# First norm and head of the input projection as one hand-ordered region

## The chip, the cores and the metric

The kernel runs on one core of a Trainium2 chip. Its time is the time of one execution on the device in microseconds (us), the median of several runs. The profile shows one execution, instruction by instruction. TensorE (PE in the rows) multiplies; VectorE (DVE), ScalarE (ACT) and GpSimd (POOL) work on elements; SyncE (SP) here only issues loads.

## The reference, cut to what matters

The reference is a decoder trunk of two layers on an input of 512 tokens by 1024 channels, float32. Each layer normalizes its input, projects it onto the columns of four token mixers, runs these, projects back and adds; then it normalizes again, runs a gated convolutional feed-forward net, and adds. The part around the change is the first layer's start:

```
def rmsnorm(x, g):
    xf = x.astype(jnp.float32)
    y = xf * lax.rsqrt(jnp.mean(xf * xf, axis=-1, keepdims=True) + RMS_EPS)
    return (y * g).astype(x.dtype)
...
def reference(x, norm_mix, w_in, ...):
    for l in range(DEPTH):
        h = rmsnorm(x, norm_mix[l])
        proj = h @ w_in[l]
        pa, pb, pc, pd = split_cols(proj, [NSA_COLS, DIL_COLS, RWKV_COLS, CONV_COLS])
        ...
        x = x + jnp.concatenate([y_a, y_b, y_c, y_d], axis=-1) @ w_out[l]
        h = rmsnorm(x, norm_ffn[l])
        x = x + conv_ffn(h, ffn_up[l], ffn_dw[l], ffn_dw_b[l], ffn_down[l])
    return rmsnorm(x, norm_final)
```

## The kernel before, in words

Channels lie on the 128 partitions, so x is eight tiles of 128 channels by 512 tokens. Products are made in float16 from pairs: a weight tile is split into a high and a low part by ScalarE and VectorE (`_split`, L200 and L201), the normalized x into two parts likewise (`norm_apply`, L401 to L403), and `mm3` (L221 to L223) adds three products of the parts. An output tile of 128 channels takes 8 x 3 products of 512 columns.

The first norm works by halves of 256 tokens. `norm_add` squares each tile of x on ScalarE and adds the squares into two accumulators on VectorE and GpSimd. `norm_rb` sums the accumulators over channels with products by ones (L383), takes one over the root in ten small steps of VectorE (`rsqrt_cols`, L256 to L267), and spreads it over the channels with transposes (L387). `norm_apply` scales x, converts to the high part and subtracts for the low part. `gemm_head` makes the first four output tiles by halves of the tokens, in four banks of PSUM (two of a ring named g, two of a ring of three named r), and leaves them in `stash`, from which `rwkv_in` takes them. Evacuation of a bank is one operation of ScalarE and one of VectorE (L411, L412). The fifth tile needs a bank of the ring g again.

Staged weights have two buffers (`wst`), split weights five (`whl`). `next_w` keeps two weights ahead. x, one weight and the small tables are loaded in `run` under a raised priority, all of x through SyncE's queue; `layer_params` issues three small loads from ScalarE's queue and derives 12 small tables on GpSimd from the loaded parameters.

The order of each engine's instructions is not the order of the program: a planner draws it up with a model of the durations (`schedule_with_timeline_sim=True`), by priority and dependence. So loads, splits and products of different stages are interleaved, and parts of the second layer's parameters are loaded early.

## Time and profile before

| | us |
|---|---|
| median of three timed runs | 1356.83 |
| lowest and highest of them | 1355.47, 1357.44 |
| span of the profiled execution (first to last instruction) | 1353.0 |
| TensorE busy (share of the span) | 1301.1 (96%) |
| VectorE busy | 910.4 (67%) |
| ScalarE busy | 609.3 (45%) |
| GpSimd busy | 119.5 (9%) |

The profiled execution's own time is not given apart from its span; the timed runs lie 2.5 to 4.4 us above the span, their median 3.8. Busy time is the sum of the durations that the profile shows; products on TensorE overlap, and their ends are modelled, so a busy TensorE is not one at its peak. The spacing of two starts tells more of its pace than a duration.

### The profile page before, as it was taken

The numbers are of one execution on the slowest core, as the hardware profiler recorded it, in microseconds if no ns is written. First come the engines' busy times: TensorE is split into PE (matmuls) and PEld (weight loads), VectorE is DVE, ScalarE is ACT, GpSimd is POOL, SyncE is SP. The second block draws the span as 40 slices with busy tenths as digits, with TensorE's granted clock in tenths as the row PEclk, the third lists the DMA queues.
The fourth block names the chain that finished last, engine by engine and source line by source line (L and its number), as shares of the span: only waits on it lengthen the run. The fifth ranks groups of instructions, "written<-read, shape, count | busy, mean of one in ns | idle before, by whom it ended". The sixth has DMA issues, their size and how long they took to land.

```text
span 1353.0 us, 22896 instructions
## 1 busy us (share of the span) xinstructions
PE 1301.1 (96%) x9198; PEld 737.9 (55%) x9198; DVE 910.4 (67%) x1770; ACT 609.3 (45%) x1115; POOL 119.5 (9%) x180
## 2 busy tenths in 40 slices
PE   5999999999999999999999998999999999999996
PEld 4545567656644444444674455775584444444445
DVE  6779985777777777632277899757678677774323
ACT  5544567644544444422245345766345444443220
POOL 2000022213000000001100001223110000000110
PEclk9999989999999999999999999999999999999998
DMA  6521400022233233333333223001214333333321
GB/s 221 162 79 59 125 26 10 1 71 94 93 94 109 93 109 94 102 120 118 109 129 124 66 79 102 10 3 32 78 49 128 105 103 100 106 93 102 98 86 63
DMA packets 41866, 119.97 MB, mean 89 GB/s; under 512 B 4896, under 2 KB 11680, under 8 KB 41760
## 3 DMA queue, kind: packets, MB, share of 16 engines
q1 hardware_dynamic: 35136, 110.50, 26.2%
q10 hardware_dynamic: 6624, 8.01, 1.8%
q8 instruction: 72, 1.18, 0.4%
q14 instruction: 34, 0.28, 0.1%
HBM read 114.30 MB, written 4.19 MB: 88 GB/s over the span
## 4 chain that ended last, share of the span: by engine, by line
PE 77%; DVE 15%; ACT 3%; DMA 2%; issue 2%; SPq 0%; ACTq 0%; DVEq 0%
PE g L222 20%; PE g L223 20%; PE g L221 20%; DVE cacc L733 4%; DVE hl L201 3%; PE v L900 3%; PE t L889 2%; PE s L869 2%; PE r L556 1%; DMA st<-in_wi_dram 1%; ACT hl L200 1%; PE r L222 1%; PE r L223 1%; DVE e L872 1%; PE r L221 1%
## 5 line engine op out<-in xcount | busy, mean ns | idle before, releaser
L221 PE MATMUL g<-hx,hl 128*128 128x512 f16 (+1 forms) x1024 | 373.7, 368 | 4.2 <-ACT hx L402 3.7
L222 PE MATMUL g<-hx,hl 128*128 128x512 f16 (+1 forms) x1024 | 374.5, 368 | 1.0 <-DVE hx L403 0.9
L201 DVE SCALAR_TENSOR_TENSOR hl<-st,hl 128x1024 f16<-128x1024 f32 (+2 forms) x200 | 239.9, 1199 | 201.0 <-ACT hl L200 200.7
L223 PE MATMUL g<-hx,hl 128*128 128x512 f16 (+1 forms) x1024 | 374.9, 368 | 0.0
L200 ACT ACTIVATE hl<-st 128x1024 f16<-128x1024 f32 (+2 forms) x200 | 206.0, 1031 | 272.7 <-PE g L223 227.7
L221 PEld LDWEIGHTS <-hl 128*128 128x128 f16 x1724 | 170.6, 99 | 162.9 <-issue 7.5
L223 PEld LDWEIGHTS <-hl 128*128 128x128 f16 x1724 | 169.8, 98 | 157.8 <-issue 2.4
L222 PEld LDWEIGHTS <-hl 128*128 128x128 f16 x1724 | 170.2, 99 | 155.2 <-issue 2.9
L222 PE MATMUL g<-act,hl 128*128 128x512 f16 (+1 forms) x396 | 140.7, 355 | 0.0
L223 PE MATMUL g<-act,hl 128*128 128x512 f16 (+1 forms) x396 | 140.7, 355 | 0.0
L221 PE MATMUL g<-act,hl 128*128 128x512 f16 (+1 forms) x396 | 140.7, 355 | 0.0
L733 DVE SCALAR_TENSOR_TENSOR cacc<-gl,d_cdw,cacc 128x511 f32<-128x511 f32 (+14 forms) x120 | 89.8, 748 | 1.4
L370 POOL TENSOR_TENSOR acc<-acc,sq 128x256 f32<-128x256 f32 (+1 forms) x38 | 44.0, 1157 | 465.9 <-ACT sq L363 409.8
L887 POOL TENSOR_SCALAR e<-e,den 128x512 f32<-128x512 f32 (+3 forms) x96 | 55.9, 596 | 316.6 <-DVE den L879 208.0
L1006 DVE SCALAR_TENSOR_TENSOR x<-g,x 128x512 f32<-128x512 f32 (+1 forms) x62 | 34.9, 568 | 67.2 <-PE g L223 67.2
L1089 ACT CAST act<-u 128x512 f16<-128x512 f32 x44 | 27.2, 618 | 114.0 <-DVE u L1087 114.0
L872 DVE CUSTOM_DVE_ANT_0 e<-s,con 128x512 f32<-128x512 f32 (+3 forms) x96 | 46.7, 487 | 33.7 <-PE s L869 25.0
L1085 ACT ACTIVATE fth<-u 128x512 f32<-128x512 f32 x44 | 27.6, 628 | 82.9 <-DVE u L1082 82.9
L1082 DVE SCALAR_TENSOR_TENSOR u<-g,d_fdw,u 128x510 f32<-128x510 f32 x84 | 62.8, 748 | 2.7
L1080 ACT ACTIVATE u<-g,par,d_fdw 128x512 f32<-128x512 f32 x84 | 64.0, 762 | 0.0
L1081 DVE SCALAR_TENSOR_TENSOR u<-g,d_fdw,u 128x511 f32<-128x511 f32 x84 | 62.5, 744 | 0.0
L876 ACT ACTIVATE e<-e,mx 128x512 f32<-128x512 f32 (+3 forms) x96 | 53.2, 556 | 16.2 <-DVE mx L874 16.1
(265 smaller groups left out, 1634.3 us busy)
## 6 DMA issues: line engine op xcount, KB each, us to landing
st<-in_up_dram SPq DMA_DIRECT2D x88, 512.0 KB, 3.5
st<-in_wi_dram SPq DMA_DIRECT2D x40, 512.0 KB, 3.4
st<-in_dn_dram SPq DMA_DIRECT2D x32, 512.0 KB, 3.5
st<-in_wo_dram SPq DMA_DIRECT2D x16, 512.0 KB, 3.5
st<-in_dn_dram SPq DMA_DIRECT2D x16, 384.0 KB, 3.1
w<-in_cw_dram ACTq DMA_DIRECT2D x16, 256.0 KB, 4.1
st<-in_wv_dram SPq DMA_DIRECT2D x8, 396.0 KB, 3.1
x<-in_x_dram SPq DMA_DIRECT2D x16, 128.0 KB, 3.5
```

What stands on the lines that cost most here:

```text
L200: nc.scalar.activation(hl[:, 0, :cols], st[:, :cols], AF.Copy, scale=SW)
L201: nc.vector.scalar_tensor_tensor(hl[:, 1, :cols], st[:, :cols], SW, hl[:, 0, :cols], op0=ALU.mult, op1=ALU.subtract)
L221: nc.tensor.matmul(ps, hl[:, 0, w], hx[:, 0, cols], start=start, stop=False)
L222: nc.tensor.matmul(ps, hl[:, 0, w], hx[:, 1, cols], start=False, stop=False)
L223: nc.tensor.matmul(ps, hl[:, 1, w], hx[:, 0, cols], start=False, stop=stop)
L733: nc.vector.scalar_tensor_tensor(acc[:, s:512], gl[:, 0:512 - s], wj, acc[:, s:512], op0=ALU.mult, op1=ALU.add)
L872: nc.vector.tensor_tensor_reduce(es[i], ps[:, o:o + w], mask[:, 384 - 128 * t:512], op0=ALU.add, op1=ALU.max, scale=1.0, scalar=-3e38, acc ...
L876: nc.scalar.activation(es[i], es[i], AF.Exp, scale=SC, bias=mx[:, i:i + 1], accum_out=den[:, i:i + 1])
L887: nc.gpsimd.tensor_scalar(es[i], es[i], den[:, i:i + 1], 1.0, op0=ALU.mult, op1=ALU.mult)
L1080: nc.scalar.activation(u, ps, AF.Identity, scale=w[:, 88 + ch:89 + ch], bias=self.p("fb", ch))
L1081: stt(u[:, 1:512], ps[:, 0:511], w[:, 44 + ch:45 + ch], u[:, 1:512], op0=ALU.mult, op1=ALU.add)
L1082: stt(u[:, 2:512], ps[:, 0:510], w[:, ch:ch + 1], u[:, 2:512], op0=ALU.mult, op1=ALU.add)
```

## The change: what it does

`run` no longer loads x under raised priority and calls `norm_add` and `norm_apply`; it calls a new function, `open_x`, inside `tc.manual_schedule()`, within which each engine takes its instructions in the order of the program. In this region:

- The first halves of x are loaded by SyncE and ScalarE in turn. The first four weights have a staging buffer each (`st0`), all four loaded by SyncE between and behind the halves of x. The rest of the constants follows there, and the three small loads of `layer_loads` come at the region's end.
- 44, 28 and 8 products of a tile of zeros with itself are put on TensorE (`spin`): before the first half's sums, between them and the transposes, and behind the transposes.
- In the first half four squares are added by VectorE and two go straight to TensorE's sum. In the second half the six additions are on GpSimd.
- The subtractions of the second and fourth tile in the first half go to GpSimd.
- The first half's products go through two weights at once, then the third and the fourth; the second half's norm lies between. The second half's products go by tiles of x, all four weights for each.
- The first split behind the region is ordered behind the region's last conversion (ScalarE) and subtraction (VectorE).

`norm_rb` is cut into `norm_sums` and `norm_spread`, `_split` into `split_hi` and `split_lo`, `layer_params` into three, with the same instructions; the other changed lines are comments. The core of the diff:

```
     def gemm_head(self, hx, n):
+        if self.stash:
+            return
...
     def _split(self, src, cols):
-        nc.scalar.activation(hl[:, 0, :cols], st[:, :cols], AF.Copy, scale=SW)
-        nc.vector.scalar_tensor_tensor(hl[:, 1, :cols], st[:, :cols], SW, hl[:, 0, :cols],
-                                       op0=ALU.mult, op1=ALU.subtract)
+        first = self.split_hi(hl, st, cols), self.split_lo(hl, st, cols)
+        if self.opened is not None:
+            for later, earlier in zip(first, self.opened):
+                self.order(later, earlier)
+            self.opened = None
...
-        if l == 0:
-            self.nc.sync.dma_start(self.con[:, 128:], self.a["con"][:, 128:])
...
-            with tc.high_priority():
-                for i, cols in enumerate(self.HALVES):
-                    for k in range(NK):
-                        nc.sync.dma_start(self.x[k][:, cols], a["x"][:, k, cols])
-                    if i == 0:
-                        nc.sync.dma_start(self.con[:, :128], a["con"][:, :128])
-                        self.load_par(0)
-                    for _ in range(W_AHEAD):
-                        self.ready.append(self._split(*self.todo.pop(0)))
-            self.layer_params(0)
-            self.norm_begin(ip, 4, 2)
-            for cols in self.HALVES:
-                for k in range(NK):
-                    a1 = k % 3 == 1
-                    self.norm_add(k, cols, nc.gpsimd if a1 else nc.vector, int(a1))
-                self.norm_apply(self.d["gm"], hx, cols)
+            with tc.manual_schedule():
+                self.open_x(ip, hx)
...
+    def open_x(self, ip, hx):
+        nc, a = self.nc, self.a
+        h0, h1 = self.HALVES
+        load = lambda eng, k, cols: eng.dma_start(self.x[k][:, cols], a["x"][:, k, cols])
+        for k in range(NK):
+            load((nc.sync, nc.scalar)[k % 2], k, h0)
+        items = [self.todo.pop(0) for _ in range(HEAD)]
+        st = []
+
+        def w_in():
+            src, cols = items[len(st)]
+            t = ip.tile([128, 1024], F32, tag="st0", bufs=HEAD, name=self.n("st"))
+            nc.sync.dma_start(t, src)
+            st.append(t)
+
+        w_in()
+        nc.sync.dma_start(self.con[:, :128], a["con"][:, :128])
+        self.load_par(0)
+        w_in()
+        for k in range(NK):
+            load(nc.sync, k, h1)
+        w_in()
+        w_in()
+        nc.sync.dma_start(self.con[:, 128:], a["con"][:, 128:])
+        self.layer_consts()
+
+        idle = self.vbank()
+
+        def spin(n):
+            for _ in range(n):
+                nc.tensor.matmul(idle[:, 0:128], self.zero, self.zero, start=True, stop=True)
+
+        spin(44)
+        self.norm_begin(ip, 6, 2)
+        for k in range(NK):
+            self.norm_add(k, h0, nc.vector if k < NK - 2 else None, k % 2)
+        ps = self.norm_sums(h0)
+        spin(28)
+        hls = [self.whl.tile([128, 2, 1024], F16, tag="hl", name=self.n("hl")) for _ in range(HEAD)]
+        hi = lambda i: self.split_hi(hls[i], st[i], 1024)
+        lo = lambda i: self.split_lo(hls[i], st[i], 1024)
+
+        hi(0)
+        rb = self.norm_spread(ps, h0)
+        spin(8)
+        pss = [self.gbank() if i < BG else self.rbank() for i in range(HEAD)]
+
+        def mm(i, k, cols):
+            self.mm3(pss[i][:, cols], hls[i], k, hx[k], cols, k == 0, k == NK - 1)
+
+        def apply(rb, cols, pool, after):
+            nts = []
+            for k in range(NK + 1):
+                if k < NK:
+                    nts.append(self.norm_mul(k, self.d["gm"], rb, cols))
+                    act = nc.scalar.copy(hx[k][:, 0, cols], nts[k])
+                if k:
+                    dve = (nc.vector, nc.gpsimd)[k - 1 in pool].tensor_tensor(
+                        hx[k - 1][:, 1, cols], nts[k - 1], hx[k - 1][:, 0, cols], op=ALU.subtract)
+                    after(k - 1)
+            self.opened = act, dve
+
+        def first(k):
+            if k == 0:
+                lo(0)
+                hi(1)
+            if k == 2:
+                lo(1)
+            for i in {3: (0,), 4: (1, 2), 5: (3, 4), 6: (5, 6, 7)}.get(k, ()):
+                self.norm_add(i, h1, nc.gpsimd, i % 2)
+
+        apply(rb, h0, (1, 3), first)
+        for k in range(NK):
+            for i in range(2):
+                mm(i, k, h0)
+        for i in range(2, HEAD):
+            hi(i)
+            lo(i)
+        for k in range(NK):
+            mm(2, k, h0)
+        self.spread_done = None
+        ps = self.norm_sums(h1)
+        for k in range(NK // 2):
+            mm(3, k, h0)
+        rb = self.norm_spread(ps, h1)
+        for k in range(NK // 2, NK):
+            mm(3, k, h0)
+        apply(rb, h1, (), lambda k: None)
+        for k in range(NK):
+            for i in range(HEAD):
+                mm(i, k, h1)
+        self.layer_loads(0)
+        self.stash = pss
```

## Rows read from the trace of the kernel before

**Rows 1.** The page's first part: busy time, share of the span, instructions.
```profile
PE 1301.1 (96%) x9198; PEld 737.9 (55%) x9198; DVE 910.4 (67%) x1770; ACT 609.3 (45%) x1115; POOL 119.5 (9%) x180
```

**Rows 2.** Waits of TensorE, 45 to 1330 us: total, times, longest; first, last of 14.
```profile
PE v L936 <- DVE ec L933: 4.5, 2, 2.4
...
PE r L278 <- ACT yw L274: 0.2, 1, 0.2
```

**Rows 3.** Busy time by windows: PE, PEld, DVE, ACT, POOL, granted clock, DMA share, GB/s.
```profile
20.00:25.00 5.00, 5.00 (x34) 3.92 (x34) 4.96 (x17) 3.44 (x6) 0.00 (x0) 1.00 0.43 138
```

**Rows 4.** Timeline of TensorE, 8 to 48 us: start, duration, line, out<-in, idle before.
```profile
8.80 1.87 PE L383 MATMUL s<-ones,acc 128*128 128x1 f32 x8 [7.01 <-DVE acc L370]
16.28 0.69 PE L387 MATMUL t<-con,y 128*128 128x128 f32 x2 [5.62 <-DVE y L267]
...
20.09 0.42 PE L223 MATMUL g<-hx,hl 128*128 128x256 f16 x1
20.30 0.42 PE L221 MATMUL g<-hx,hl 128*128 128x256 f16 x1
...
22.86 0.28 PE L222 MATMUL g<-hx,hl 128*128 128x256 f16 x1
...
42.19 0.27 PE L223 MATMUL r<-hx,hl 128*128 128x256 f16 x1
42.30 0.38 PE L221 MATMUL g<-hx,hl 128*128 128x512 f16 x1
```

**Rows 5.** Timeline, 0 to 10 us: loads issued, and ScalarE's table load and last squares.
```profile
0.74 4.72 SPq L1178 DMA_DIRECT2D x<-in_x_dram  x8
...
1.66 0.45 ACTq L324 DMA_DIRECT2D pos<-in_pos_dram  x1
2.15 1.28 ACT L363 ACT_TABLE_LOAD   x1 [2.15 <-issue]
...
7.87 0.75 ACT L363 ACTIVATE sq<-x 128x256 f32<-128x256 f32 x2 [0.77 <-DMA x<-in_x_dram]
```

**Rows 6.** Timeline, 10 to 17 us: the root's steps, and an addition beside GpSimd's.
```profile
10.70 0.16 DVE L256 TENSOR_SCALAR u<-s 128x2 f32<-128x2 f32 x1 [1.96 <-PE s L383]
...
11.72 0.23 DVE L263 SCALAR_TENSOR_TENSOR y<-a,y 128x2 f32<-128x2 f32 x1
...
14.62 0.72 POOL L370 TENSOR_TENSOR acc<-acc,sq 128x256 f32<-128x256 f32 x1 [1.54 <-ACT sq L363]
...
14.78 0.85 DVE L370 TENSOR_TENSOR acc<-acc,sq 128x256 f32<-128x256 f32 x1
...
16.07 0.15 DVE L267 SCALAR_TENSOR_TENSOR y<-a,y 128x2 f32<-128x2 f32 x1
```

**Rows 7.** Timelines of ScalarE and VectorE: pace of squares, low parts, scalings, conversions, subtractions.
```profile
13.53 1.63 ACT L363 ACTIVATE sq<-x 128x256 f32<-128x256 f32 x5
...
27.80 1.23 DVE L201 SCALAR_TENSOR_TENSOR hl<-st,hl 128x1024 f16<-128x1024 f32 x1 [0.80 <-ACT hl L200]
...
30.16 1.26 DVE L401 SCALAR_TENSOR_TENSOR nt<-x,d_gm,t 128x256 f32<-128x256 f32 x3 [0.73 <-PE t L387]
30.68 1.19 ACT L402 CAST hx<-nt 128x256 f16<-128x256 f32 x3 [2.61 <-DVE nt L401]
31.35 0.75 DVE L403 TENSOR_TENSOR hx<-nt,hx 128x256 f16<-128x256 f32 x2
```

**Rows 8.** Timelines: weight load of zeros, and a later norm's sums.
```profile
16.55 0.15 PEld L378 LDWEIGHTS <-zero 128*128 128x128 f16 x1
...
323.16 0.50 PE L383 MATMUL s<-ones,sq 128*128 128x1 f32 x4
```

**Rows 9.** Timelines of ScalarE and VectorE: first evacuation, and a split behind it.
```profile
39.86 0.67 ACT L411 ACTIVATE wa<-g,d_om 128x512 f32<-128x512 f32 x1
40.43 1.05 ACT L200 ACTIVATE hl<-st 128x1024 f16<-128x1024 f32 x1
...
41.13 0.74 DVE L412 SCALAR_TENSOR_TENSOR wa<-g,d_mu,wa 128x511 f32<-128x511 f32 x1
```

More of the change, by code (lines that the diff above doesn't have):

```diff
@@ L191, in w_split @@
     def w_split(self, src, cols):
-        nc = self.nc
         with self.tc.high_priority():
@@ L196, in _split, with split_hi, split_lo @@
     def _split(self, src, cols):
-        nc = self.nc
         st = self.w_load(src, cols)
         hl = self.whl.tile([128, 2, 1024], F16, tag="hl", name=self.n("hl"))
-        nc.scalar.activation(hl[:, 0, :cols], st[:, :cols], AF.Copy, scale=SW)
-        nc.vector.scalar_tensor_tensor(hl[:, 1, :cols], st[:, :cols], SW, hl[:, 0, :cols],
-                                       op0=ALU.mult, op1=ALU.subtract)
-        return hl
+        first = self.split_hi(hl, st, cols), self.split_lo(hl, st, cols)
+        if self.opened is not None:
+            for later, earlier in zip(first, self.opened):
+                self.order(later, earlier)
+            self.opened = None
+        return hl
+    def split_hi(self, hl, st, cols):
+        return self.nc.scalar.activation(hl[:, 0, :cols], st[:, :cols], AF.Copy, scale=SW)
+    def split_lo(self, hl, st, cols):
+        return self.nc.vector.scalar_tensor_tensor(hl[:, 1, :cols], st[:, :cols], SW, hl[:, 0, :cols],
+                                                   op0=ALU.mult, op1=ALU.subtract)
     def plan(self, items, depth):
@@ L314, in layer_params, with ptile, layer_loads @@
     def layer_params(self, l):
-        nc, a = self.nc, self.a
-        t = lambda name, shape: self.cp.tile(shape, F32, tag=name, bufs=1, name=self.n(name))
-        if l:
-            self.load_par(l)
+        self.load_par(l)
+        self.layer_loads(l)
+        self.layer_consts()
+    def ptile(self, name, shape):
+        return self.cp.tile(shape, F32, tag=name, bufs=1, name=self.n(name))
+    def layer_loads(self, l):
+        nc, a, t = self.nc, self.a, self.ptile
         self.lora = t("lora", [128, 512])
@@ L324, in layer_params, with layer_consts @@
         nc.scalar.dma_start(self.pos, a["pos"][l])
-        v = nc.gpsimd
+    def layer_consts(self):
+        t = self.ptile
+        v = self.nc.gpsimd
         self.d = {}
@@ L373, in norm_rb, with norm_sums @@
         nc = self.nc
-        ps, rb = self.sbank(), self.tbank()
+        return self.norm_spread(self.norm_sums(cols), cols)
+    def norm_sums(self, cols):
+        nc = self.nc
+        ps = self.sbank()
         sqs = self.accs + self.direct
@@ L384, in norm_rb, with norm_spread @@
                                  start=False, stop=i == len(sqs) - 1 and t == n // 128 - 1)
+        return ps
+    def norm_spread(self, ps, cols):
+        nc = self.nc
+        rb = self.tbank()
+        n = cols.stop - cols.start
         y = self.rsqrt_cols("n", ps, n // 128, 1.0 / D, 1e-6)
@@ L394, in order, with norm_mul @@
             mybir.DependencyClass.NoSync, mybir.DependencyReason.DATA), reason="order")
+    def norm_mul(self, k, g, rb, cols):
+        t = self.np.tile([128, 256], F32, tag="nt", bufs=3, name=self.n("nt"))
+        self.nc.vector.scalar_tensor_tensor(t, self.x[k][:, cols], g[:, k:k + 1], rb, op0=ALU.mult, op1=ALU.mult)
+        return t
     def norm_apply(self, g, hx, cols):
@@ L399, in norm_apply @@
         for k in range(NK):
-            t = self.np.tile([128, 256], F32, tag="nt", bufs=3, name=self.n("nt"))
-            nc.vector.scalar_tensor_tensor(t, self.x[k][:, cols], g[:, k:k + 1], rb, op0=ALU.mult, op1=ALU.mult)
+            t = self.norm_mul(k, g, rb, cols)
             nc.scalar.copy(hx[k][:, 0, cols], t)
@@ L1214, in run @@
                         self.norm_apply(self.d["gm"], hx, cols)
+    def open_x(self, ip, hx):
[20 more added lines that the diff above has]
+        nc.sync.dma_start(self.con[:, 128:], a["con"][:, 128:])
+        self.layer_consts()
+        idle = self.vbank()
[58 more added lines that the diff above has]
+        self.stash = pss
```

## The prediction

> **What bounds the kernel now.** I read the page first: TensorE is busy for 96% of the span [rows 1], so a change pays only where it takes time out of TensorE's queue. The list of TensorE's waits inside the body, from 45 to 1330 us, has 14 rows that add up to 25.1 us, the longest group 4.5 us in two waits [rows 2]. The rest of TensorE's idle time lies at the two ends. So I went on to the timeline of the first 48 us. There the reader is to see three stretches. Until 20 us TensorE does nothing but two sums of squares and two pairs of transposes: it waits 7.0 us for the squares and 5.6 us for the root [rows 4]. From 20.09 the products of the first four output tiles follow each other without a hole until 42.30, when the fifth tile begins. In this stretch the 256-column products start 0.21 us apart at first and 0.11 us apart from about 22.9 us on. That is TensorE's two levels, 1.2 and 2.4 GHz, although the granted clock of 20 to 25 us reads 1.00 [rows 3, 4]: here I trust the spacing. What it did before the rise was dense products since 20.09, after some thin work.
>
> The yardstick is therefore one moment: the start of the fifth tile, 42.30 us. What comes later is not edited. The span is 1353.0 us and the median of the timed runs 1356.83, so some 3.8 us lie around the span; I carry them over unchanged.
>
> **The loads of x.** Before, SyncE issues the eight first halves in 4.72 us, 0.59 apart, and the last squares end at 8.62 [rows 5]. The last load was issued near 4.87, its square started near 8.2: 3.3 us from issue to use. Now four go through SyncE (the last at 0.74 + 3 x 0.59 = 2.51) and four through ScalarE's queue, where an issue took 0.45 and three ended at 2.11. The last x is there at 2.51 + 3.3 = 5.8. ScalarE's four issues end near 2.6, its table load takes 1.28, so squares start at 3.9; eight at 0.30 (five take 1.63, [rows 7]) end at 6.4 if nothing waits. I take 6.7: 1.9 us earlier than before. The three small tables that filled ScalarE's queue go to the end of the region, 1.4 us of issues behind the last conversion; they are wanted after the fifth tile, so that costs nothing. SyncE's later loads, the region's 4.2 MB of x and weights in all, are issued by 11 us at that spacing (17 issues behind 2.51, 0.5 each), and the third and fourth weight are wanted only near 20 us.
>
> **Products of zeros and sums of squares.** 44 products of 128 columns stand in TensorE's queue before the sums. The trace shows none back to back. Half the spacing of a 256-column product gives 0.107 us; the weight load of zeros takes 0.15 [rows 8], and if nothing overlaps one costs 0.26. So they end at 1.6 + 4.7 = 6.3, at 8.2, or at 13. I take the first, because in the dense stream the weight loads lie beside the products. The sums now have four operands in place of two: 16 records instead of 8. Eight took 1.87 us at the slow level [rows 4], four took 0.50 at the fast one, of which some 0.15 lies under the next product (a 256-column product lasts 0.27 at a spacing of 0.11) [rows 4, 8]. That is 3.7 or 1.5 us. With the clock risen by then, the sums end at 8.4; without, at 10.3.
>
> By the Trainium skill (TensorE: Matmul & The Clock Gate, "Back-to-back issue gap") a stream of 128-column products with their weight loads keeps about 81 ns each at the fast level. By it the 28 zero products behind the sums would take 2.3 us and hold the transposes back by 0.2 us, an estimate that I leave out of the sum; no run here shows it yet.
>
> **The root.** Six of its ten VectorE steps ran from 10.70 to 11.95, so ten take 2.05; but in the old order the weight's low part and additions came between, and the last ended at 16.22 [rows 6]. That interruption of 3.4 us goes. The root is ready at 10.5, the transposes (0.69 slow, half of it fast) end at 10.9. Before, they ended at 16.97. So the norm of the first half is 6.1 us earlier; call this moment t0.
>
> **What is late next.** The low parts of the weights, which the old order had made in the gap. VectorE's queue now holds four scalings (0.40), two subtractions (0.34) and two low parts (1.2) before the second weight is whole, with 0.4 of waits for ScalarE: t0 + 5.1. TensorE, in order, stands at the second tile's third product until then. The two tiles' 48 products then take 5.2 us at the fast level and are paced by the conversions to t0 + 9.8; if as many of them run at the slow level as did before, some 18 at 0.21, they end at t0 + 12.1. Between t0 - 1 and t0 + 5 TensorE does hardly 1.5 us of work, so I expect the slow level there. It matters little, since the third weight is late as well: ScalarE has eight conversions (0.39), the second high part (1.05), eight squares (0.30) and the third high part, 7.6 us, and some 3 us of waits for VectorE among them: t0 + 10.6, and the low part behind it t0 + 11.9. The third tile then ends at t0 + 14.6.
>
> Six additions of the second half's squares now stand on GpSimd, 0.72 each. A VectorE addition that began beside one of them took 0.85, more than two subtractions of that size in a row (0.75) [rows 6, 7], so they shut each other out: from the third square at t0 + 7.3, with two subtractions and two low parts between, they end near t0 + 14.6, just when TensorE comes to the sum. Unhindered they would end at t0 + 11.6.
>
> The rows show this of additions alone. The Trainium skill (SBUF — State Buffer, "SBUF: two separate sides") says which operations it holds for: VectorE's with two operands in SBUF against GpSimd's, each locked out for the whole of the other. By it the subtractions and the low parts of the weights lock as well and the scalings, with one operand in PSUM, do not; without it the additions on GpSimd would be 3 us earlier, and TensorE would still wait for the third weight, so the sum stays.
>
> Then 0.75 of sums, and the root (2.05) and transposes (0.35) beside 12 products (1.3): 0.75 idle. Twelve more, and the second half's 96 products at 0.109 run from about t0 + 19.7 to t0 + 30.4. Sum: 10.9 + 30.4 = 41.3.
>
> **The end of the region.** The old order finished the four tiles one after the other; now all four end in the last 1.3 us. The fifth tile needs the first one's bank, which is free after ScalarE's and VectorE's evacuation (0.67 and 0.74, [rows 9]). The first bank's last product is 0.98 before the end, so TensorE stands still for 0.5. If a weight's parts (1.05 and 1.2) are put ahead of the evacuation, which the old order also did, it is up to 2.0. I take 0.55: start of the fifth tile at 41.85 against 42.30, a gain of 0.45 us. That the rest of the order is drawn up anew by the planner I price at zero, with bounds from the waits it can move: one of the longest groups more or less, 4.5 us either way [rows 2].
>
> So the span becomes 1352.5 and the time 1356.4 us: the first norm comes 6.1 us earlier, and nearly all of it goes again in waits for weights, a late second norm and a bank. About 0.2%, 2.7 us, is what a measurement of this kernel can tell from no change.
>
> **Rivals.**
> The head gains more. If ScalarE and VectorE keep tighter than I count, the third weight is not late and the clock stays up, the second half ends near t0 + 27 = 37.9, and with 0.55 the gain is 3.9: 1353.0. For it: the zero products around the root. Against: ScalarE's queue as counted.
> The planner's new order of the body loses one of the long groups of waits: -0.45 - 4.4 gives 1352.0. Nothing in the profile speaks for it beyond the fact that such waits are few and single.
> The products of zeros stand in the way (slower). At 0.15 each they end at 8.2, and if the clock has not risen the sums take 3.7: 11.9 instead of 8.4, 3.5 later, and the transposes 0.35 more: 1360.2. It decides from 3.2 us on. For it: 0.15 of weight load at the slow level; against: dense products from 20.09 had brought the rise by 22.9 in the old order, and these start at 1.6.
> The bank (slower). Two weights' parts ahead of the first evacuation, and the second bank in the same queue: 4.5 us of standing instead of 0.55, 1360.3; it decides above 3.7. For it: a high part before the second evacuation at 40.43 [rows 9]; against: only one staging buffer is full by then.
> The change doesn't do what it says: that is nearly my forecast, the head ends when it did.
>
> **Chances.** Forecast 0.44 (own range 1354.4 to 1358.8), tighter head 0.17, better body 0.15, zeros in the way 0.11, bank or a worse body 0.13. Faster takes the two good cases, same the forecast, slower the two bad ones, with a little of each across the bounds: 0.33, 0.43, 0.24. The range 1351.6 to 1360.6 reaches the four rivals.
>
> **What would show it.** Right: squares done near 6.7, first transposes ended near 10.9, TensorE waiting on low parts of weights between 12 and 16 and again before the third tile, a hole of about half a microsecond before the fifth tile, and that tile starting within 1.5 us of 42.3. Wrong: first transposes after 13, the 256-column products 0.11 apart from 12 us on without holes, or waits in the body whose sum differs by more than 3 us.

## The result and the profile after

The changed kernel takes 1367.53 us (median of 4 runs, 1366.43 to 1370.56); the kernel before, run beside it, 1357.12. The ratio is 1.0088, 95% interval 1.0070 to 1.0106: slower by some 10 us where no change was forecast, and outside the range of the prediction.

The profiled run took 1368.60 us for a span of 1366.6; before, the span was 1353.0. The start of the fifth tile, the prediction's yardstick, and the four stretches behind it divide the 13.6 us between them. A stretch ends where the sums of the next norm are first read by VectorE.

| stretch, us | before | after | difference |
|---|---|---|---|
| to the fifth tile | 42.30 | 50.85 | +8.55 |
| first layer, mixers | 281.41 | 285.36 | +3.95 |
| first layer, feed-forward | 350.52 | 350.52 | 0 |
| second layer, mixers | 311.99 | 311.64 | -0.35 |
| second layer, feed-forward, and end | 366.78 | 368.23 | +1.45 |

So the head lost 8.55 us by itself, and the part that nobody edited, from here on "the body", lost 5.05. What lies around the span is 2.0 us in this run, not the 3.8 that the prediction carried over; by that the profile of before, with 1353.0, belongs to a run of about 1355.0. By the medians (+10.4) the body's share is 1.9.

TensorE's busy share is the same 96% [rows 1], and that tells nothing:

```profile
PE 1313.5 (96%) x9286; PEld 745.8 (55%) x9286; DVE 910.1 (67%) x1764; ACT 608.7 (45%) x1115; POOL 127.9 (9%) x184
```

**The loads.** The timeline of the changed kernel, first 20 us, DMA issues and ScalarE, then TensorE (start, duration, engine and line, out<-in; in brackets the idle time before and what ended it); it answers to [rows 4, 5]:

```profile
0.74 0.86 SPq L189 DMA_DIRECT2D st<-in_wi_dram  x2
1.65 4.20 SPq L1237 DMA_DIRECT2D x<-in_x_dram  x4
...
0.73 6.68 ACTq L1237 DMA_DIRECT2D x<-in_x_dram  x4
7.44 1.28 ACT L381 ACT_TABLE_LOAD   x1 [7.44 <-DMA st<-in_wi_dram]
...
9.37 1.94 ACT L381 ACTIVATE sq<-x 128x256 f32<-128x256 f32 x6
...
10.95 1.87 PE L405 MATMUL s<-ones,acc 128*128 128x1 f32 x8 [5.24 <-DVE acc L388]
12.68 1.85 PE L405 MATMUL s<-ones,sq 128*128 128x1 f32 x8
14.39 3.15 PE L1264 MATMUL v<-zero 128*128 128x128 f16 x28
17.33 0.63 PE L415 MATMUL t<-con,y 128*128 128x128 f32 x2
```

The reader is to see the first row. L189 is `w_load`: two weights of 512 KB, not of the region at all but of the fifth and sixth tile, stand at the head of SyncE's queue. The program issues them behind the region; the planner drew them ahead, since their staging buffers were free and nothing held them back. Everything behind them is late. The waits of SyncE's queue in the first 19 us (total, times, longest):

```profile
SPq L1237 <- DMA st<-in_wi_dram: 4.1, 3, 2.0
```

The trace names what holds an issue. All 290 transfers of the program signal their landing on eight semaphores, those of both queues together, and an issue that takes a semaphore again first waits until the transfer that had it has landed. So eight are in flight at most. Here the ninth and the tenth issue are the last x on SyncE's and on ScalarE's queue, and the semaphores that they take are those of the two weights. Timelines of SyncE (5 to 6 us) and ScalarE (6 to 7.4), and the time from issue to landing of the two weights (`--tile st`, 0 to 2 us):

```profile
5.52 0.33 SPq L1237 DMA_DIRECT2D x<-in_x_dram  x1
...
7.08 0.34 ACTq L1237 DMA_DIRECT2D x<-in_x_dram  x1
...
DMA to landing us min/median/max: 4.8/5.3/5.9
```

The weights were issued at 0.74 and 1.18 and landed at 5.50 and 7.06; each held issue follows 0.02 us behind a landing. So the four issues of x on ScalarE's own queue end at 7.41; the table load and the squares stand behind them, and the squares then follow each other without a wait. They end at 11.31, against 8.62 before and a forecast of 6.7. The loads of x also land late by themselves (the first at 5.67, in e1 below at 3.46); what the hold and what the shared transfer is worth is not told apart. The products of zeros had ended at 5.71, so TensorE then stood for 5.24 us, and the windows (columns as in [rows 3]; the number behind the five engines is the granted clock) show what followed:

```profile
5.00:10.00 5.00, 0.71 (x14) 0.59 (x11) 0.20 (x1) 2.55 (x6) 0.00 (x0) 0.81 0.84 275
10.00:15.00 5.00, 4.05 (x23) 4.05 (x24) 1.60 (x7) 2.36 (x6) 1.79 (x9) 0.50 1.00 304
```

From 10 to 15 us the granted clock is 0.50, the level of 1.2 GHz, though TensorE is busy for 4.05 of the 5 us: the 16 sums take 1.87 and 1.85 us and the 28 zeros 3.15.

**The bank.** The timeline around the fifth tile, ScalarE, VectorE, TensorE:

```profile
47.73 1.06 ACT L207 ACTIVATE hl<-st 128x1024 f16<-128x1024 f32 x1 [4.21 <-PE g L231]
48.70 0.67 ACT L443 ACTIVATE wa<-g,d_om 128x512 f32<-128x512 f32 x1
...
49.96 0.74 DVE L444 SCALAR_TENSOR_TENSOR wa<-g,d_mu,wa 128x511 f32<-128x511 f32 x1
...
50.85 0.38 PE L229 MATMUL g<-hx,hl 128*128 128x512 f16 x1 [2.18 <-DVE wa L444]
```

The planner put the sixth tile's split ahead of the first evacuation on both engines, 1.06 and 1.23 us, and the fifth tile waits 2.18.

**The body.** Waits of TensorE behind the head, 54 to 1340 us (total, times, longest); the same list as [rows 2], now 17 rows that add up to 28.3 us in place of 25.1:

```profile
PE v L968 <- DVE ec L965: 4.3, 2, 2.6
...
PE g L229 <- DVE u L1114: 2.2, 2, 1.6
...
PE r L288 <- ACT yw L284: 1.3, 2, 1.1
```

Before, the wait for `yw` was 0.2 [rows 2] and the one for `u` 0.6, in a row between those shown. Of the body's 5.05 us in this pair of profiles 3.2 are such waits.

### The profile page after: what moved, and what is told of

It reads as the page before. It is cut to its first block, busy times and chain, and to the rows that moved or that the text cites. A ratio compares the mean times of both kernels' runs of the same rounds, so it can differ in the third digit from the quotient of the medians.

```text
span 1366.6 us, 23065 instructions
## 1 busy us (share of the span) xinstructions
PE 1313.5 (96%) x9286; PEld 745.8 (55%) x9286; DVE 910.1 (67%) x1764; ACT 608.7 (45%) x1115; POOL 127.9 (9%) x184
## 4 chain that ended last, share of the span: by engine, by line
PE 75%; DVE 15%; ACT 4%; DMA 3%; issue 2%; ACTq 0%; DVEq 0%; SPq 0%
PE g L230 20%; PE g L231 20%; PE g L229 20%; DVE cacc L765 4%; DVE hl L210 3%; PE v L932 3%; DMA st<-in_wi_dram 2%; PE t L921 2%; PE s L901 2%; ACT hl L207 1%; PE r L588 1%; DVE e L904 1%; PE r L230 1%; PE r L231 1%; PE r L229 1%
## 5 line engine op out<-in xcount | busy, mean ns | idle before, releaser
L388 POOL TENSOR_TENSOR acc<-acc,sq 128x256 f32<-128x256 f32 (+1 forms) x40 | 47.6, 1194 | 460.5 <-ACT sq L381 404.4
```

## The experiments

All kernels ran beside the kernel before. "Head" is the start of the fifth tile less 42.30; "time" is the median less that of before in the same series; "body" is time less head; "mixers" is the first mixer stretch of the profiled run (281.41 before).

| kernel | transposes end | fifth tile | head | time (ratio, 95% interval) | body | mixers |
|---|---|---|---|---|---|---|
| changed | 17.96 | 50.85 | +8.55 | +10.4 (1.0070 to 1.0106) | 1.9 | 285.36 |
| e1 | 11.03 | 43.36 | +1.06 | +7.8 (1.0032 to 1.0065) | 6.8 | 288.18 |
| e2 | 17.80 | 49.05 | +6.75 | +14.9 (1.0092 to 1.0125) | 8.2 | 283.91 |
| e3 | 10.72 | 41.38 | -0.92 | +4.5 (1.0024 to 1.0043) | 5.4 | 283.17 |
| e4 | 12.73 | 45.11 | +2.81 | +15.5 (1.0093 to 1.0136) | 12.6 | 288.56 |
| e5 | 15.54 | 49.16 | +6.86 | +6.6 (1.0028 to 1.0053) | -0.2 | 281.92 |
| e6 | 10.74 | 41.00 | -1.30 | +8.0 (1.0034 to 1.0064) | 9.3 | 286.66 |
| e7 | 11.64 | 41.00 | -1.30 | +4.9 (1.0027 to 1.0055) | 6.2 | 285.24 |
| e8 | 21.05 | 47.15 | +4.85 | +5.1 (1.0021 to 1.0044) | 0.3 | 282.86 |
| e9 | 11.62 | 42.58 | +0.28 | +24.1 (1.0165 to 1.0200) | 23.8 | 293.62 |
| e10 | 16.54 | 41.67 | -0.63 | +27.6 (1.0184 to 1.0228) | 28.2 | 295.28 |
| e11 | 10.60 | 40.59 | -1.71 | +20.7 (1.0131 to 1.0165) | 22.4 | 290.29 |
| e12 | 11.59 | 42.53 | +0.23 | +5.2 (1.0024 to 1.0052) | 5.0 | 284.18 |
| e14 | 11.68 | 41.03 | -1.27 | +5.1 (1.0022 to 1.0046) | 6.4 | 285.19 |
| e21 | 11.34 | 40.69 | -1.61 | +16.7 (1.0094 to 1.0145) | 18.3 | 300.06 |
| e22 | 11.23 | 41.53 | -0.77 | +3.6 (1.0023 to 1.0049) | 4.4 | 285.99 |
| e24 | 16.15 | 41.83 | -0.47 | +19.2 (1.0127 to 1.0158) | 19.7 | 299.66 |

Head and mixers are read from one profiled execution each. e3, e9, e12 and e22 have the same region and heads from -0.92 to +0.28, so a head is known to about 1 us. Runs of one kernel lie up to 7.5 us from their median (e21: 1365.49, with a median of 1373.01), and the intervals of the ratios are 1.3 to 3.5 us to either side. A body is known to some 2 to 4 us.

### e1 to e3: the loads and the bank

e1 orders every weight load of `w_load` behind the region's last load; e2 orders the second split behind the region behind the first evacuation; e3 does both.

```
-        nc.sync.dma_start(st[:, :cols], src)
+        ld = nc.sync.dma_start(st[:, :cols], src)
+        if self.last_load is not None:
+            self.order(ld, self.last_load)
...
+        elif self.second and self.evac is not None:
+            for later, earlier in zip(first, self.evac):
+                self.order(later, earlier)
```

Expected of e1: 

> The two weights that the planner drew ahead of x on SyncE's queue (fifth and sixth tile) are put behind the region's last load. Theory (those two loads are the main loss: bandwidth, and issues of x that wait for them): last squares end near 6.8 us instead of 11.3, the sums run at the fast level, first transposes end near 11 instead of 18.0, the fifth tile starts near 44 instead of 50.85, time 1360 to 1361. Rival 1 (the order by hand sets the pace, x is early enough anyway): fifth tile not before 48, time 1365 or more. Rival 2 (the loss lies in the body's new order): the fifth tile moves but the time stays within 2 us of 1367.5.

Expected of e2: 

> The second weight behind the region is split behind the evacuation of the first bank, on ScalarE and VectorE, instead of ahead of it; nothing else. Theory (the bank is the smaller loss): TensorE's wait before the fifth tile falls from 2.2 to 0.6 us, fifth tile near 49.2, time near 1366. Rival (the evacuations are what holds the whole mixer stage): time 1363 or less. No effect if the split waits for something else as well: 1367.5.

Expected of e3: 

> Both edits. Theory: the gains add, first transposes end near 11, fifth tile near 42.3 as in the kernel before, and the time is what the body's order leaves: 1357 if it costs nothing, near 1360.5 if the 3.5 us that the changed kernel loses between the fifth tile and the feed-forward norm stay. Rival (one wait hides the other): not better than the first edit alone by more than 0.5 us.

The heads came out as expected, to 0.9 us. The timeline of e1, loads, table load and transposes:

```profile
0.73 1.81 SPq L1240 DMA_DIRECT2D x<-in_x_dram  x4
...
0.73 1.86 ACTq L1240 DMA_DIRECT2D x<-in_x_dram  x4
2.62 1.28 ACT L384 ACT_TABLE_LOAD   x1 [2.62 <-issue]
...
10.60 0.43 PE L418 MATMUL t<-con,y 128*128 128x128 f32 x2 [0.45 <-DVE y L280]
```

The same four issues on ScalarE's queue take 1.86 us in place of 6.68, and the transposes end 6.9 us earlier: the two loads alone had cost 7.5 us of head. In e1 the first eight issues are the eight loads of x; the ninth, a weight, goes at 3.47, and the last x lands at 6.33 in place of 9.20. e2 took the wait for the bank from 2.18 to 0.64. e3 has both, and its head is the one that was predicted:

```profile
4.55 2.33 ACT L391 ACTIVATE sq<-x 128x256 f32<-128x256 f32 x6
...
7.22 1.03 PE L415 MATMUL s<-ones,sq 128*128 128x1 f32 x8
8.12 1.72 PE L1276 MATMUL v<-zero 128*128 128x128 f16 x28
10.29 0.43 PE L425 MATMUL t<-con,y 128*128 128x128 f32 x2 [0.45 <-DVE y L287]
...
41.38 0.38 PE L239 MATMUL g<-hx,hl 128*128 128x512 f16 x1 [0.64 <-DVE wa L454]
```

The times missed for e1 by 2.4 to 3.4 us and for e2 by 4.5; e3 came in within its range, at the slow end. With the head mended the kernel is still 4.5 us slower than before, so a third cost lies in the body.

### e4: without the zeros

e1 with an empty `spin`; the products whose results nobody reads are left out.

Expected: 

> The loads put behind, as in the first, and no products of zeros at all. Theory (the zeros are worth the level of the sums and of the first products): the 16 records of the sums take 3.7 us instead of 1.5, transposes end near 13, fifth tile near 46, time near 1362.5. Rival (the clock falls again before the real products, so the zeros change nothing that counts): fifth tile within 0.7 us of the first experiment's.

```profile
6.31 1.87 PE L408 MATMUL s<-ones,acc 128*128 128x1 f32 x8 [4.53 <-DVE acc L391]
8.04 1.85 PE L408 MATMUL s<-ones,sq 128*128 128x1 f32 x8
...
12.04 0.69 PE L418 MATMUL t<-con,y 128*128 128x128 f32 x2 [2.15 <-DVE y L280]
```

The sums take 1.87 and 1.85 us in place of 1.03 each (e3), and the fifth tile is 1.75 later than in e1. So the zeros do what the change adds them for, where they reach to the sums. In the profiles of the kernels with the loads in order they don't always: in e1, e3, e6 and e11 the first 44 end between 6.30 and 6.47, when the sums begin, and the 28 behind the sums take 1.72 us; in e7, e9, e12, e14 and e21 they end between 5.49 and 5.80, TensorE stands for 0.3 to 0.7 us before the sums, and the 28 take 2.88 to 3.15 (e22 lies between, with 2.13). The granted clock from 8 to 12 us is 1.00 in e3 and 0.61 in e12, whose region is the same; that makes most of the difference between their heads. What ends the zeros early in one profile and not in another is not shown. The time is 7.6 us worse than that of e1, of which the head explains 1.75; the rest is the body again.

### e5: a head that is only longer

The kernel before with 64 more products by zeros inside the first four tiles (which adds nothing to them), to tell a later start of the body from a different body.

```
-                    self.mm3(ps[:, cols], hl, k, hx[k], cols, k == 0, k == NK - 1)
+                    self.mm3(ps[:, cols], hl, k, hx[k], cols, k == 0, k == NK - 1 and not longer)
+                    if longer:
+                        self.nc.tensor.matmul(ps[:, cols], self.zero, hx[k][:, 0, cols], start=False,
+                                              stop=k == NK - 1)
```

Expected: 

> The kernel before, with a 256-column product of zeros added to each of the 64 steps of the first four tiles: the head alone is made 64 x 0.109 = 7.0 us longer, the planner draws up the rest as it likes. Theory (the planner's new order behind a shifted head costs time by itself): from the fifth tile to the first sum of the feed-forward norm it takes 283 to 288 us instead of 281.4, or a feed-forward stage gets its 1.7 us longer; time 7 us and 2 to 6 more. Rival (a shift of the head passes through one to one, and the body's loss in the changed kernel comes from how its region ends): that stretch stays within 0.7 us of 281.4, time 7 us more.

The head is 6.86 later and the time 6.6; the first mixer stretch keeps its length to 0.5 us. The rival holds: a shift of the head passes one to one, and is no cause of a body cost. What e5 also keeps is the order: of TensorE's first 1600 products and transposes from the first `lora` product on, all but 2 lie in the longest sequence that it shares with the kernel before, compared by the tiles that each writes and reads. In the changed kernel 21 lie outside, in e1 to e7 without e5 36 to 39.

### e6, e7: banks in turn, and zeros ahead of the first products

e6 is e3 with the last half of the second half's channels tile by tile, so that the banks come free one after the other; e7 puts 14 and 20 more zeros ahead of the first products of the first and second tile.

```
-        for k in range(NK):
+        for k in range(NK // 2):
             for i in range(HEAD):
                 mm(i, k, h1)
+        for i in range(HEAD):
+            for k in range(NK // 2, NK):
+                mm(i, k, h1)
...
+                if k == 0:
+                    spin((14, 20)[i])
                 mm(i, k, h0)
```

Expected of e6: 

> Both edits of the third experiment, and the second half's products by tile from the fifth tile of x on, so that the four banks are finished 1.3 us apart instead of in the last 1.3 us together. Theory (the common end makes the wait for the bank): no wait before the fifth tile, which starts near 40.6 instead of 41.38. If the body's loss comes from the late splits and evacuations at the common end, the stretch up to the feed-forward norm falls back to 281.5 and the time to 1356; if it comes from the planner's order, the stretch takes some other value from 281 to 288.

Expected of e7: 

> As the experiment before, and 14 and 20 more products of zeros ahead of the first products of the first and the second weight, where TensorE waits for the low parts anyway. Theory (between root and second weight the clock falls): no 256-column product at a spacing of 0.21, against 21; the first two tiles end 2 us earlier, but the third weight's low part then ends the wait, so the fifth tile moves by 0.5 to 1.0 only. Rival (the slow products are the bound): it moves by 2.2.

e6 has no wait for the bank left, and its fifth tile starts at 41.00; in its profile the wait for the second weight's low part is longer (2.5 in place of 1.6). e7 has none of the 17 to 23 products at the slow spacing that e1, e3 and e6 show, and its fifth tile starts at 41.00 too. TensorE now waits 0.29 and 0.87 for the third weight's parts, which it didn't in e6. In e7's profile the transposes also end 0.9 later than in e6, with slow zeros before them; e11, whose region is the same, has its fifth tile at 40.59. So the gain is 0.4 us or less by the start of the fifth tile, 0.9 from the transposes on, and not the rival's 2.2. That is the prediction's "the third weight is late as well", and speaks against its rival of a tighter head.

### e8: the old order with x on two queues

The odd tiles of x's first half from ScalarE's queue, nothing else.

```
-                        nc.sync.dma_start(self.x[k][:, cols], a["x"][:, k, cols])
+                        (nc.sync, nc.scalar)[k % 2 * (1 - i)].dma_start(self.x[k][:, cols], a["x"][:, k, cols])
```

Expected: 

> The kernel before with one part of the change alone: the odd tiles of x's first half are loaded from ScalarE's queue. Theory (x's arrival sets the first norm): last squares end near 7.2 instead of 8.6, first root earlier by as much or less, since a weight's low part still stands between its steps; fifth tile 0.5 to 1.5 earlier, time within 2 us of before. Rival (the first weight's arrival sets the first products): fifth tile within 0.3.

A miss: the fifth tile is 4.85 later, not earlier.

```profile
1.18 3.00 ACTq L1178 DMA_DIRECT2D x<-in_x_dram  x4
...
5.84 1.28 ACT L363 ACT_TABLE_LOAD   x1 [5.84 <-DMA x<-in_x_dram]
```

ScalarE's queue here still had the three tables to issue, its issues of x took 3.00 us, and the table load came at 5.84 against 2.15 [rows 5]. An issuing queue that is also the engine of the squares pays for each held issue. The ninth issue, a load of x on ScalarE's queue, went at 3.85, when the load of x whose semaphore it takes had landed. The body kept its order (2 of 1600) and, by the medians, its length.

### e9 to e11: the chain of the compression moved

In e3 TensorE is idle for 1.3 us some 20 to 28 us behind the fifth tile (the 3.4 in the expectation of e9 is not in this trace), among the small products of `cmp_in`, here called links, each of which needs the one before. e9 (on e3), e10 (on the kernel before) and e11 (on e7) put that chain behind the next group of tiles in the program, in both layers. The expectations from here on take the first `r<-kvr,bk`, a product of the first mixer, as a mark of time.

```
-ORDER = ("R0 CM E0 R1 E1 ...
+ORDER = ("R0 CM E0 R1 CH2 E1 ...
```

Expected of e9: 

> The kernel of e3 with the chain of the compression (its small products behind the pooled keys, each waiting for the one before) put behind the second group of tiles in the program, so that the planner lays a tile between its links. Theory, the planner's new order costs the body its time: in e3 the links stand one behind another on TensorE, 3.4 us idle and a fall of the granted clock to 0.70 some 20 to 28 us behind the fifth tile; here links 3 and 4 lie between products, the first r<-kvr,bk starts at about +58.5 behind the fifth tile (e3: 60.8, before: 57.5), the first mixer stretch is 281.4 to 282.5 (e3: 283.2), the time about 1358.5 (e3: 1360.0). Rival, the loss comes from the granted clock or late weights whatever the order: +60.5 or more, 283 to 286, 1360 or more.

Expected of e10: 

> The kernel before with the same edit alone. Theory: its chain had tiles between its links already, so nothing is to be gained: within 1 us of before, first mixer stretch 281 to 282. Rival, the edit is a gain of its own: 2 us or more faster than before, which would say nothing of the region.

Expected of e11: 

> The kernel of e7 (loads in order, banks in turn, zeros ahead of the first products) with the same edit. Theory: the first r<-kvr,bk from +62.3 to about +58.5, the first mixer stretch from 285.2 to 281.5 to 282.5, the time from 1360.0 to about 1357. Rival: 284 to 286 and 1360.

All three are 20 to 28 us slower, the kernel before too. The control makes this a failed experiment, and the most telling one: an edit that I had priced at nothing costs 28 us behind an untouched head. 304 of 1600 products lie outside the shared sequence there, but in e9 only 56, so the count does not price an order. e9 loses 12 us in each layer's mixers (293.6 and 323.6 in place of 281.4 and 312.0). Whether the late chain itself or the new order is the cost, these runs do not tell.

### e12, e14: only the last links, by an order on TensorE

The last links behind the root's transposes, where TensorE has them in the kernel before; their lines also move there in the program, for all engines. e12 is on e3, e14 on e7. The same edit in the kernel before was not run.

```
+        if self.rest is not None:
+            self.rest()
...
+            self.order(mm, self.spread_end)
```

Expected of e12: 

> The kernel of e3 with the last links of the first layer's compression ordered, on TensorE alone, behind the transposes of the first mixer's root (r<-con,yw), which gives TensorE the order that it has in the kernel before: root, link, second lora pair, a tile, link, a tile, link. Theory, the planner draws the links ahead of the root and each is waited for in the open: waits of s on ACT part, DVE hid and ACT kc gone (1.6 us with the loads behind), the granted clock 1.00 from 20 to 32 us behind the fifth tile (e3: 0.70 in one stretch), the first r<-kvr,bk at +59 or less (e3: 60.8), first mixer stretch 281.4 to 282.3 (e3: 283.2), time 1358 to 1359 (e3: 1360.0). Rival, another wait takes the place (the root itself is late because ACT and DVE are): +60.5 and 283, time 1360.

Expected of e14: 

> The kernel of e7 with the same order of the links. In e7 they lie ahead of the root on VectorE (0.6 us) and ScalarE (four copies, 0.9 us), and the root's copy yw ends the wait of TensorE. Theory: the second lora pair from +26.6 behind the fifth tile to about +24.5, the first r<-kvr,bk from +62.3 to about 59.5, first mixer stretch from 285.2 to 282 to 283, time from 1360.0 to 1357 to 1358. Rival, the tile whose weight comes late is what TensorE lacks: +61.5 or more, 284 to 286, 1360.

My theory fell. The links' waits are gone, and the wait moved to the root's copy `yw`, which feeds the transposes, as the rival of e12 said. But e14's timeline names what is ahead of it (VectorE, ScalarE, TensorE):

```profile
53.69 1.22 DVE L495 TENSOR_TENSOR_SCAN lc<-rst,lw 128x512 f32<-128x512 f32 x1
...
57.22 1.06 ACT L218 ACTIVATE hl<-st 128x1024 f16<-128x1024 f32 x1 [4.24 <-DMA st<-in_wi_dram]
58.18 0.61 ACT L498 ACTIVATE pc<-lc 128x512 f32<-128x512 f32 x1
...
59.98 1.05 PE L270 MATMUL r<-con,sq 128*128 128x2 f32 x8 [0.82 <-ACT sq L506]
...
65.02 1.11 PE L299 MATMUL r<-con,yw 128*128 128x128 f32 x4 [2.98 <-ACT yw L295]
```

`lc` is ready at 54.9, but ScalarE stands for 4.24 us before a split whose weight has not landed, and `pc` is behind it. In the kernel before, ScalarE waits for `lc` there, and TensorE for nothing:

```profile
55.90 0.63 ACT L453 ACTIVATE pc<-lc 128x512 f32<-128x512 f32 x1 [3.98 <-DVE lc L450]
...
63.41 0.66 PE L278 MATMUL r<-con,yw 128*128 128x128 f32 x4
```

And the clock goes with it. Windows of e14: TensorE busy for 1.04 of 4 us, then the level of 1.2 GHz:

```profile
61.00:65.00 4.00, 1.04 (x33) 0.77 (x32) 2.81 (x11) 1.49 (x4) 0.00 (x0) 0.72 0.54 176
65.00:69.00 4.00, 3.98 (x12) 2.04 (x13) 3.37 (x6) 1.34 (x3) 0.00 (x0) 0.50 0.16 64
```

### e21, e22, e24: that split behind the stage's square

One order on ScalarE: the first split that follows the first mixer's elementwise stage in the program comes behind that stage's square. e21 on e7, e22 on e3, e24 on the kernel before.

```
+        if self.hold is not None and self.held is None:
+            self.order(first[0], self.hold)
+            self.held = self.hold
...
+        self.hold, self.held = act(sq, k, AF.Square, scale=self.p("k_k", c)), self.held or self.hold
```

Expected of e21: 

> The kernel of e7 with one added order in the first layer: the first split that follows the first mixer's elementwise stage in the program (the eighth tile's weight) comes on ScalarE behind that stage's square sq<-k, so the later splits do too. In e7 and e14 seven splits stand ahead of the exponential pc, the last of them waits 4.2 us for its load, and pc, sq, the sums, the root's copy yw and the evacuation of the sixth tile's bank follow it, so TensorE stands. Theory, splits drawn ahead of that stage cost the region's kernels their body time: sq by about +14 behind the fifth tile (e7: 18), second lora pair at about +22 (e7: 26.6), the first r<-kvr,bk at 57.5 to 59 (e7: 62.3), first mixer stretch 281 to 282.5 (e7: 285.2), time about 1356.5 (e7: 1360.0). Rival, TensorE runs out of work there whatever stands on ScalarE: 61.5 or more, 284 to 286, 1360.

Expected of e22: 

> The kernel of e3 with the same added order. Theory: the first r<-kvr,bk at 58 to 59.5 behind the fifth tile (e3: 60.8), first mixer stretch 281 to 282.5 (e3: 283.2 in its profile), time about 1357.5 (e3: 1360.0). Rival: 60.5 or more, 283 to 286, 1360.

Expected of e24: 

> The kernel before with the same added order alone: there the exponential waits for VectorE, not for a split (pc 3.98 us behind lc), so theory expects next to nothing: within 1 us of before, first r<-kvr,bk at 57 to 58.5, first mixer stretch 281 to 282. If it gains 2 us or more the order is a gain of its own and says less about the region.

At that place the theory holds. e21, ScalarE and TensorE, and the window that answers to the first of e14's:

```profile
51.05 0.63 ACT L501 ACTIVATE pc<-lc 128x512 f32<-128x512 f32 x1 [2.60 <-DVE lc L498]
...
59.88 0.60 PE L302 MATMUL r<-con,yw 128*128 128x128 f32 x4
```

```profile
61.00:65.00 4.00, 4.00 (x27) 1.58 (x27) 4.00 (x6) 1.63 (x2) 0.00 (x0) 1.00 0.43 147
```

`pc` waits for its data and not for a weight, the root's transposes wait for nothing, the clock stays at 2.4 GHz, and the first `r<-kvr,bk` starts 57.5 us behind the fifth tile, as before (57.5), against 62.3 in e7. So 4.8 us came back at that place. But the order drawn around it moves 291 of 1600 products, and some 20 us are lost later in the same stretch (300.06 against 285.24, with 4.8 gained at its start): e21 is 12 us slower than e7. e24 shows the same loss with the old head: 299.66 in e24, 300.06 in e21. In e22 the stage is early as well (second pair of `lora` at +19.8 against +24.9 in e3), another wait takes its place (2.95 for the evacuation of `k`), and the time is that of e3 within the noise.

The trace also shows what the later loss is made of. The first mixer stretch before and in e21 (columns as in [rows 3]), and TensorE's two longest waits in e21's, neither of which is among those of before:

```profile
42.30:323.71 281.41, 272.40 (x2571) 167.62 (x2569) 218.02 (x520) 150.02 (x341) 42.77 (x68) 0.99 0.21 66
...
40.69:340.75 300.06, 281.24 (x2571) 170.53 (x2569) 219.98 (x518) 150.58 (x340) 43.67 (x68) 0.96 0.20 64
...
PE r L578 <- DVE S L607: 2.9, 4, 1.8
PE r L738 <- DVE Y L736: 2.9, 2, 1.6
```

TensorE stands still for 18.8 us in place of 9.0, and for the same 2571 records it is busy 8.8 us longer, at a mean granted clock of 0.96 in place of 0.99. So this order costs twice: about half of the 18.7 us are waits, the other half products at the lower level.

## Why the prediction was wrong

The head was forecast at 41.85 and came at 50.85. By the prediction's steps:

| step | forecast | changed | e3 |
|---|---|---|---|
| last squares end | 6.7 | 11.31 | 6.88 |
| sums end | 8.4 | 14.53 | 8.25 |
| transposes end | 10.9 | 17.96 | 10.72 |
| from there to the end of the head's products | 30.4 | 30.71 | 30.02 |
| wait for the bank | 0.55 | 2.18 | 0.64 |
| fifth tile | 41.85 | 50.85 | 41.38 |

**The step that failed** is "four go through SyncE (the last at 0.74 + 3 x 0.59 = 2.51) and four through ScalarE's queue ... The last x is there at 2.51 + 3.3 = 5.8", and with it "ScalarE's four issues end near 2.6". It took the program's order inside the region for the order of the queue. A region drawn by hand fixes the order of what is in it; it keeps nothing out, and two loads from behind it came first. ScalarE's issues ended at 7.41 and the last x landed at 9.20. That is 7.06 of the 9.0 us, and e1 takes it away. Two of the prediction's signs of being wrong came with it: transposes behind 13 us (17.96), and waits in the body that differ by more than 3 us (3.2).

The row behind that step was misread as well. The 4.72 us for eight issues [rows 5] are not a pace of 0.59 but five issues 0.47 apart, a hold, and three more; the two timelines of before, 0.7 to 3.1 and 3.5 to 4.5 us:

```profile
0.74 2.29 SPq L1178 DMA_DIRECT2D x<-in_x_dram  x5
...
4.18 0.33 SPq L1178 DMA_DIRECT2D x<-in_x_dram  x1
```

With the three small loads on ScalarE's queue these are the first eight, and the ninth goes when the first of those, `lora`, has landed at 4.16. So the limit of eight could be seen before. The smaller slips cost nothing: even in e3 the last x lands at 6.33 and not at 5.8, and the later loads (15 issues, not 17) go out by 12.87 and not 11, still ahead of their use. The rivals had a slow clock at the sums, at 1360.2, but from zeros that run too long; here it came from zeros that ended too early, 5.24 us before the sums.

**The bank** was seen as a mechanism ("If a weight's parts (1.05 and 1.2) are put ahead of the evacuation, which the old order also did, it is up to 2.0") and sized wrongly: 0.55 was taken, 2.18 measured, and e2 with 0.64 shows the cause. The argument against it, that only one staging buffer would be full by then, was wrong: both were, in e1 too, where the wait is 2.18 again.

**The body** was priced at zero with 4.5 us to either side. In the changed kernel it is 1.9 by medians and 5.05 by the profiles; with the loads in order (e1, e3, e6, e7, e12, e14, e22) 4 to 9. The bound was worked out from single waits of the list, and that was the wrong place: an order moves many of them at once. e5 and e8, whose order is that of before but for 2 products, show bodies within 0.3 us by the medians; every kernel whose order moved has a slower one, up to 28 us, with the old head (e10, e24) as with the new. That the order is the cause is read from this agreement; which of the moved instructions cost the changed kernel and e3 their time is not shown.

**What held.** The root in 2 us without an interruption, the waits for low parts, the late third weight, GpSimd's late additions, and the sum from the transposes on (30.4 against 30.0 to 30.7; the second weight whole at t0 + 5.05 in e3 against 5.1, the third tile ended at t0 + 14.4 against 14.6). So the verdict that the head's 6 us would nearly all go again was right: in e3 the first norm ends 6.25 us earlier than before and the fifth tile starts 0.92 earlier. That e3's 41.38 lies so near the forecast 41.85 is in part luck: e12 with the same region has 42.53, with slow zeros before the transposes.

The estimate from the Trainium skill (TensorE: Matmul & The Clock Gate, "Back-to-back issue gap"), 2.3 us for 28 products of zeros at 81 ns, does not agree: they took 1.72 us in e3, 61 ns each, and 3.15 us at the slow level in the changed kernel; the measurement decides, and the sum did not hang on it.

**Open.** Which order of the body would keep both the early head and the 281.4 us. The first loss, in e7 and e14, is named and was removed at its place by e21; the losses later in the stretch that came with e21's order are seen as waits and clock, but not traced to an instruction, nor are the changed kernel's 1.1 us for `yw` and 1.6 for `u` beyond the rows. To pin the old body's order behind the new head was not tried. No kernel here beats the one before.

## What to carry to other kernels

A region with an order of its own is no fence: list what the planner may draw ahead of it, above all loads whose buffers are free, and order those behind the region's last load; count the loads in flight, for a large one ahead holds back small ones on the other queue too. When a change moves where a planned part begins, price the redrawn part by a control, one harmless order in the old kernel, and not by the waits that can be seen; if the control swings by more than the gain, the gain is not to be had without fixing that order. Do not let an engine issue loads that its own first instructions stand behind.

## What the runs showed of the hardware

- Four issues of x on ScalarE's queue took 1.86 us with nothing else ahead (e1), 3.00 behind a table (e8), and 6.68 with two weights of 512 KB ahead on SyncE's queue (changed kernel). The difference is no cost of issuing but the program's wait for one of its eight semaphores: in all kernels here at most eight transfers are in flight, and the first held issue follows a landing by 0.02 us (3.47 in e1, 3.85 in e8, 5.52 in the changed kernel).
- VectorE and GpSimd shut each other out for more than additions. In e3 a subtraction on GpSimd that starts 0.1 us behind the low part of a weight ends 0.5 us behind that part's end and lasts 1.65. In e6 two such subtractions start ahead of VectorE's next and take 0.74 each, and there the low part that begins during the second lasts 1.68 in place of 1.22. The six additions take 6.52 us where one took 0.72 [rows 6]. The rule that the prediction took from the Trainium skill (SBUF — State Buffer, "SBUF: two separate sides") says this of such pairs; these rows agree with it:

```profile
12.13 1.22 DVE L220 SCALAR_TENSOR_TENSOR hl<-st,hl 128x1024 f16<-128x1024 f32 x1
...
12.23 1.65 POOL L1303 TENSOR_TENSOR hx<-nt,hx 128x256 f16<-128x256 f32 x1
...
17.92 6.52 POOL L398 TENSOR_TENSOR acc<-acc,sq 128x256 f32<-128x256 f32 x6 [1.62 <-ACT sq L391]
```

and e6:

```profile
14.14 1.48 POOL L1303 TENSOR_TENSOR hx<-nt,hx 128x256 f16<-128x256 f32 x2
...
15.02 1.68 DVE L220 SCALAR_TENSOR_TENSOR hl<-st,hl 128x1024 f16<-128x1024 f32 x1
```

- The granted clock fell to 0.50 after 5.24 us of idle TensorE (changed kernel) and after 3.0 of waiting in 4 us (e14), and with it the four `lora` products behind the root went from 1.1 us (e21, 60.41 to 61.54) to 2.1 (e14, 66.33 to 68.42).
